# Staging the operands of a down-projection: two tiles and one row buffer, later calls, low parts on VectorE

## The chip, the core and the metric

One core of one Trainium2 chip runs the whole program. The metric is device time in microseconds; the kernel before took 2233.93 us, the median of 3 runs.

## What is computed

A trunk of two layers over 1040 tokens (16 meta tokens ahead of 1024), 1024 channels, in float32. Layer 0 mixes tokens with a gated short convolution, layer 1 with a gated linear recurrence; behind each stands a gated MLP (FFN, inner width 2816) with a convolution of width 3 between up-projection and activation.

```python
def short_conv_mixer(x, w_in, conv_w, w_out):
    b_gate, c_gate, v = jnp.split(x @ w_in, 3, axis=-1)
    return (b_gate * causal_dwconv(c_gate * v, conv_w)) @ w_out

def rglru_block(...):
    g_branch, r_branch = jnp.split(x @ w_in, 2, axis=-1)
    u = causal_dwconv(r_branch, conv_w) + conv_b
    # r, i: sigmoid gates of u by block-diagonal weights
    # a = exp(-8 r softplus(-lam)); hs = scan of a, sqrt(1-a*a) * i * u
    return (hs * gelu(g_branch)) @ w_out

def conv_gated_mlp(x, w_up, conv_w, w_down):
    g, v = jnp.split(causal_dwconv(x @ w_up, conv_w), 2, axis=-1)
    return (silu(g) * v) @ w_down

for layer in range(2):
    h = h + mixer[layer](rms_norm(h))
    h = h + conv_gated_mlp(rms_norm(h))
out = rms_norm(h)[:, 16:]
```

## The kernel before

Channels lie in partitions, tokens in columns, 1040 in four banks of 260. Each float32 product is made of three matmuls in the fp32r type: an operand is split into a high part, cast by ScalarE, and a low part, the difference, so that high x high, high x low and low x high are summed in PSUM. Weights are split so by split_weights (L225 to L229: cast L227, subtract L228 on VectorE). SyncE loads them, mostly 256 or 512 KB at a time; run() and its helper ahead (L290 to L312) make the split pieces up to six ahead of the product that uses them, and load up to nine ahead.

There are four stages: short convolution (sc), FFN 0 (zff0), recurrent block (rg, zrg), FFN 1 (zff1). Each has an up-projection (up, L398 to L504) and a down-projection (down, L507 to L616). An up-projection goes unit by unit, a unit being two output tiles of 128 channels; most units take seven products p = 1 to 7 (in the way of Strassen) in the order 1, 2, 6, 5, 7, 4, 3, with product 1 of the next unit between 7 and 4. Each is 24 matmuls. Products 1, 6, 7, 4 add up in one bank pair "a", which ScalarE copies out on the way (L461, L465, L468), 2 in "b" and 5, 3 in "c" (VectorE, L473 among them). So product 4 can begin only when the copy L468 has read the bank behind product 7; in the last unit no product of another unit stands between these two. What a unit yields, convolved and gated, is written to DRAM (the tensors zsc, zff, zrg). PSUM holds four such tiles.

A down-projection takes its operands back, in groups of k: 8 in the short convolution, 5 and 5 in the recurrent block, 9, 7, 6 and 9, 10, 3 in the two FFNs, 62 in all. bring(k) (L515 to L523) issues a DMA on GpSimd's queue from DRAM into a staging tile, casts the high part on ScalarE (L521) and subtracts the low part on GpSimd (L522). Staging tiles are s13 and s24 (one buffer each, which the up-projection's weights use too, through L261 on the same queue) and a buffer "zs" from the pool of nine rows that the convolutions, gates and results use as well. The first group's k all go to rows; from the second group on k modulo 3 chooses. The calls that bring the first group, two k each, are hooked in after the products of the last unit, from product 1 on; the rest are brought within the group before, one per step. pair (L539 to L569) then makes two output tiles over a group: its results leave PSUM by VectorE's copies (L565, first group) or adds (L563), and a GpSimd DMA (L567) adds the residual. Recurrent gates (L780 to L804) take a matmul per bank (L790), sigmoids (L793) and other ScalarE functions, then on VectorE a chain L798, L802, the scan L803 and the product L804, whose result goes to DRAM (zrg); the tenth is made inside the first group of its down-projection.

The order on TensorE is the program's own; that on the other engines is set by the tile framework's scheduler, and each engine runs its instructions in that order. A DMA issue that waits for its buffer holds back what stands behind it on its queue.

Of the kernel before, what the change touches and what calls it, by code (L numbers as in the profile page):

```python
# [7 lines left out]
FP32 = mybir.dt.float32  # L8
F32R = mybir.dt.float32r
AF = mybir.ActivationFunctionType  # L10
ALU = mybir.AluOpType
# [22 lines left out]
NJ = KD // 2  # L34
# [35 lines left out]
def unit_order(u0, n):  # L70


    out = [(u0, 1)]
    for u in range(u0, n):
        out += [(u, p) for p in (2, 6, 5, 7)]
        if u < n - 1:
            out.append((u + 1, 1))
        out += [(u, p) for p in (4, 3)]
    return out
# [57 lines left out]
def trunk_kernel(ctx: ExitStack, tc: tile.TileContext, xt: bass.AP, small: bass.AP, ws: bass.AP, out: bass.AP):  # L137
    nc = tc.nc
# [11 lines left out]
    def row(name, dtype=FP32):  # L150
        return rpool.tile([P, T], dtype, tag="row", name=name, padded_shape=[P, T + 4])
# [16 lines left out]
    def col(name, i):  # L168
        at, n = SMALL[name]
        return cv[:, at + i:at + i + 1]  # L170
# [5 lines left out]
    rn = keep.tile([P, T], FP32, name="rn")  # L176
# [54 lines left out]
    def staging(tag):  # L231
        return wpool.tile([P, T], FP32, tag=tag, name=tag, bufs=1)
# [18 lines left out]
    def unit_pieces(q):  # L251


        st = {}

        def load(p):
            if p == 1:
                st[11] = fetch(q, 3 * C, C)
                st["s13"] = staging("s13")
                nc.sync.dma_start(st["s13"][:, :2 * C], block(q)[:, 2 * C:4 * C])  # L260
                nc.gpsimd.dma_start(st["s13"][:, :2 * C], block(q)[:, C:3 * C], accum_op=ALU.add)  # L261
            elif p == 2:
                st[12] = fetch(q, 0, C)
            elif p == 4:
                st[22] = fetch(q, C, C)

        def make(p):
            if p == 6:
                s24 = st["s24"] = staging("s24")
                nc.vector.tensor_add(s24[:, :C], st["s13"][:, :C], st[11])  # L270
                nc.vector.tensor_add(s24[:, C:2 * C], s24[:, :C], st[12])
            src = {
                1: lambda: st[11], 2: lambda: st[12], 4: lambda: st[22],
                5: lambda: st["s13"][:, :C], 7: lambda: st["s13"][:, C:2 * C],
                6: lambda: st["s24"][:, :C], 3: lambda: st["s24"][:, C:2 * C],
            }[p]()
            return split_weights(src, C)

        return {p: (lambda p=p: load(p), lambda p=p: make(p)) for p in ORDER}
# [4 lines left out]
    def step(pieces, fn):  # L284
        program.append((pieces, fn))

    def hook(fn):
        program.append((None, fn))

    def run():  # L290
        pieces = []
        for ps, _ in program:
            pieces += [p for p in ps or () if p not in pieces]
        made, state = {}, {"loaded": 0, "made": 0}

        def ahead(i, last, loads=9, makes=6):
            while state["loaded"] < min(max(i + loads, last + 1), len(pieces)):
                pieces[state["loaded"]][0]()
                state["loaded"] += 1
            while state["made"] < min(max(i + makes, last + 1), len(pieces)):  # L300
                p = pieces[state["made"]]
                made[p] = p[1]()
                state["made"] += 1

        for q, (ps, fn) in enumerate(program):
            if ps is None:
                fn()
                continue
            if ps:
                at = [pieces.index(p) for p in ps]  # L310
                ahead(min(at), max(at), *((3, 2) if min(at) < NJ - 1 else (5, 4) if min(at) < NJ else ()))
            fn(*[made[p] for p in ps])  # L312


# [83 lines left out]
    def up(name, layer, units, tok, n_plain, new_out, finish, between=lambda u: None, in_last=(), n_late=0, before_pair=lambda j: None, after_plain=lambda js: None):  # L398


        a, n = tok
# [30 lines left out]
        def product(u, p, w):  # L432
            which = {1: "a", 6: "a", 7: "a", 4: "a", 2: "b", 5: "c", 3: "c"}[p]
            first, last = p in (1, 2, 5), p in (4, 2, 3)
            if first:
                bank[u, which] = banks()
            ps = bank[u, which]
            hi, lo = w
            for j in range(NJ):
                c = slice(j * P, (j + 1) * P)  # L440
                xh, xl = X[p, j]
                for b in range(2):
                    t = slice(b * n, (b + 1) * n)
                    for r, (wt, x) in enumerate(((hi, xh), (hi, xl), (lo, xh))):
                        nc.tensor.matmul(  # L445
                            ps[:, b, :n], lhsT=wt[:, c], rhs=x[:, t],
                            start=(first and j == 0 and r == 0), stop=(last and j == NJ - 1 and r == 2),
                            skip_group_check=True,
                        )
            with tc.high_priority():  # L450
                take(u, p)
# [23 lines left out]
        def finish_unit(u):  # L475
            for k in "abc":
                bank.pop((u, k), None)
            finish(u, *(t for t, _ in outs.pop(u)))
# [9 lines left out]
                    hook(lambda: after_plain(range(2, NJ)))  # L488
        pieces = {u: unit_pieces(qs[u]) for u in range(n_plain, len(units))}
        calls = list(in_last)  # L490
        for u, p in unit_order(n_plain, len(units)):
            step((pieces[u][p],), lambda w, u=u, p=p: product(u, p, w))
            if u == len(units) - 1 and len(calls) > n_late:
                hook(calls.pop(0))
            if (u, p) == (n_plain, 6):
                yield
                for v in range(n_plain):
                    between(v)
                    hook(lambda v=v: finish_unit(v))
            if p == 3:  # L500
                between(u)
                hook(lambda u=u: finish_unit(u))
# [4 lines left out]
    def down(name, layer, groups, zd, tok, residual, ready, at=lambda g, m: None):  # L507


        a, n = tok  # L510
        e = a + 4 * n
        z, h = {}, {}
        starts = [sum(groups[:g]) for g in range(len(groups) + 1)]

        def bring(k):  # L515
            which = 2 if k < groups[0] else k % 3
            s = row("zs") if which == 2 else staging(("s13", "s24")[which])
            nc.gpsimd.dma_start(s[:, a:e], zd[k][:, a:e])
            hi = xpool.tile([P, 4 * ALL[1]], F32R, tag="x", name="zh")
            lo = xpool.tile([P, 4 * ALL[1]], F32R, tag="x", name="zl")  # L520
            nc.scalar.copy(hi[:, a:e], s[:, a:e])  # L521
            nc.gpsimd.tensor_sub(lo[:, a:e], s[:, a:e], hi[:, a:e].bitcast(FP32))  # L522
            z[k] = hi, lo  # L523

        def bring_some(ks):
# [281 lines left out]
    def add_gates(i):  # L807
# [6 lines left out]
        at=lambda g, m: add_gates(NR - 1) if (g, m) == (0, 0) else None,  # L814
# [2 lines left out]

    def give_out(m, h, t, c):
        last = c == 3
        engine = nc.vector  # L820
        engine.scalar_tensor_tensor(h[m][:, t], h[m][:, t], col("g_fin", m), rn[:, t], op0=ALU.mult, op1=ALU.mult)  # L821
        queue = (nc.sync, nc.scalar)[m % 2] if last else nc.sync
        queue.dma_start(out[:, m, t.start - N_META:t.stop - N_META], h[m][:, t])

# [83 lines left out]
```

## Time and profile before

| what | value |
|---|---|
| median of 3 runs (lowest, highest) | 2233.93 us (2231.8, 2234.08) |
| the profiled execution | 2231.59 us, span 2229.8 us |
| mean granted TensorE clock | 0.982 |
| TensorE (PE) busy | 2130.3 us, 96% of the span |
| VectorE (DVE) busy | 1491.7 us, 67% |
| ScalarE (ACT) busy | 999.0 us, 45% |
| GpSimd (POOL) busy | 322.7 us, 14% |
| DMA, mean | 116 GB/s |

The profiled execution lies 0.1% below the median. Busy times are sums over the span; the stages differ, so the waits have to be read where they stand. The line of the clock, PEclk, gives the granted clock in tenths of full; 2.4 GHz is full, and the other level is 1.2 GHz.

### The profile page before, as it was taken

How to read it: one execution, taken by the hardware profiler on the slowest of the kernel's cores; microseconds unless marked ns; L12 is line 12 of the kernel's file. 1: busy time of each engine (PE TensorE's matmuls, PEld its weight loads, DVE VectorE, ACT ScalarE, POOL GpSimd, SP SyncE). 2: the span in 40 equal slices, each digit the busy share in tenths (PEclk: the TensorE clock that was granted, in tenths of full speed). 3: DMA queues.
4: the chain of work that ended last, by engine and by line, in shares of the span. 5: the costliest groups of instructions: out<-in, count | busy, mean ns of one | idle time of the engine just before them, and what ended most of it. 6: DMA issues, size and time to landing. Idle time of an engine off the chain costs nothing. (4 is left out here: it accounts for less than half of the span.)

```text
span 2229.8 us, 41117 instructions
## 1 busy us (share of the span) xinstructions
PE 2130.3 (96%) x17364; PEld 2117.0 (95%) x17364; DVE 1491.7 (67%) x1796; ACT 999.0 (45%) x1437; POOL 322.7 (14%) x316
## 2 busy tenths in 40 slices
PE   8999999899999989999999997899999999989998
PEld 8999999899999989999999997899999999889998
DVE  8866755787788774224877776497877877853226
ACT  8433343544444442112568886174444444522113
POOL 0000410000000044220001124200000000343102
PEclk9999999999999999999999999999999999989999
DMA  5434544344444454442223334632444444544312
GB/s 175 109 108 116 172 120 111 91 116 117 121 122 114 115 189 129 122 105 72 92 74 107 100 103 121 143 128 77 118 128 115 119 109 128 176 129 122 95 34 77
DMA packets 99546, 257.61 MB, mean 116 GB/s; under 512 B 11040, under 2 KB 19104, under 8 KB 99360
## 3 DMA queue, kind: packets, MB, share of 16 engines
q1 hardware_dynamic: 76320, 172.52, 23.2%
q0 software_dynamic: 22320, 81.73, 17.4%
q8 instruction: 136, 2.23, 0.4%
q10 hardware_dynamic: 720, 0.73, 0.1%
q14 instruction: 50, 0.41, 0.1%
HBM read 205.20 MB, written 49.73 MB: 114 GB/s over the span
## 5 line engine op out<-in xcount | busy, mean ns | idle before, releaser
L445 PE MATMUL ps<-x,whi 128*128 128x260 f32 (+1 forms) x6832 | 1248.0, 285 | 38.7 <-ACT cin L468 20.6
L445 PEld LDWEIGHTS ps<-x,whi 128*128 128x128 f32 x6832 | 1067.0, 190 | 41.2 <-ACT cin L468 21.4
L445 PE MATMUL ps<-x,wlo 128*128 128x260 f32 (+1 forms) x3416 | 972.0, 285 | 0.0
L445 PEld LDWEIGHTS ps<-x,wlo 128*128 128x128 f32 x3416 | 649.9, 190 | 0.0
L228 DVE TENSOR_TENSOR wlo<-wraw,whi 128x512 fp32r<-128x512 f32 (+1 forms) x337 | 276.5, 824 | 434.5 <-ACT whi L227 434.5
L555 PE MATMUL ps<-zh,whi 128*128 128x260 f32 (+2 forms) x1888 | 537.1, 284 | 27.9 <-DVE h L565 17.6
L555 PE MATMUL ps<-zl,whi 128*128 128x260 f32 (+2 forms) x1888 | 535.6, 284 | 0.0
L555 PE MATMUL ps<-zh,wlo 128*128 128x260 f32 (+2 forms) x1888 | 535.4, 284 | 0.0
L227 ACT CAST whi<-wraw 128x512 fp32r<-128x512 f32 (+1 forms) x337 | 203.2, 606 | 603.2 <-PE ps L555 367.5
L555 PEld LDWEIGHTS ps<-zh,whi 128*128 128x128 f32 x1888 | 359.2, 190 | 29.8 <-DVE h L565 12.3
L555 PEld LDWEIGHTS ps<-zl,whi 128*128 128x128 f32 x1888 | 359.3, 190 | 0.0
L555 PEld LDWEIGHTS ps<-zh,wlo 128*128 128x128 f32 x1888 | 359.1, 190 | 0.0
L227 ACT CAST whi<-s 128x512 fp32r<-128x512 f32 x244 | 150.5, 618 | 263.2 <-PE ps L445 191.8
L261 POOL DMA_DIRECT2D s<-in_ws x61 | 53.0, 868 | 1217.8 <-DMA s<-in_ws 520.0
L623 DVE SCALAR_TENSOR_TENSOR t<-cin,cv,t 128x1040 f32<-128x1040 f32 (+1 forms) x176 | 222.8, 1325 | 8.7 <-ACT t L742 6.8
L228 DVE TENSOR_TENSOR wlo<-s,whi 128x512 fp32r<-128x512 f32 x244 | 173.1, 714 | 45.5 <-ACT whi L227 45.0
L742 ACT ACTIVATE t<-cin,cv 128x1040 f32<-128x1040 f32 (+1 forms) x88 | 97.4, 1152 | 88.0 <-DVE cin L739 88.0
L418 PE MATMUL ps<-x,whi 128*128 128x260 f32 (+1 forms) x640 | 117.0, 285 | 8.6 <-ACT whi L227 8.6
L522 POOL TENSOR_TENSOR zl<-zs,zh 128x1040 fp32r<-128x1040 f32 (+2 forms) x41 | 111.3, 2724 | 74.8 <-ACT zh L521 61.7
L739 DVE SCALAR_TENSOR_TENSOR cin<-cin,rn 128x1040 f32<-128x1040 f32 (+1 forms) x88 | 109.2, 1244 | 0.1
L418 PEld LDWEIGHTS ps<-x,whi 128*128 128x128 f32 x640 | 99.9, 191 | 8.6 <-ACT whi L227 8.6
L418 PE MATMUL ps<-x,wlo 128*128 128x260 f32 (+1 forms) x320 | 91.1, 285 | 0.4 <-DVE wlo L228 0.4
(131 smaller groups left out, 1842.3 us busy)
## 6 DMA issues: line engine op xcount, KB each, us to landing
wraw<-in_ws SPq DMA_DIRECT2D x317, 256.0 KB, 3.3
s<-in_ws SPq DMA_DIRECT2D x61, 512.0 KB, 3.6
s<-in_ws POOLq DMA_DIRECT2D x61, 512.0 KB, 5.8
zff<-t SPq DMA_DIRECT2D x22, 520.0 KB, 2.7
zff<-t SPq DMA_DIRECT2D x22, 512.0 KB, 2.7
h<-h SPq DMA_DIRECT2D x16, 520.0 KB, 3.4
zs<-zff POOLq DMA_DIRECT2D x13, 520.0 KB, 5.0
zs<-zff POOLq DMA_DIRECT2D x13, 512.0 KB, 6.1
```

The costliest lines, as they stand in the source:

```text
L227: nc.scalar.copy(hi[:, :n], src)
L228: nc.vector.tensor_sub(lo[:, :n], src, hi[:, :n].bitcast(FP32))
L261: nc.gpsimd.dma_start(st["s13"][:, :2 * C], block(q)[:, C:3 * C], accum_op=ALU.add)
L418: nc.tensor.matmul(ps[:, s, :n], lhsT=wt, rhs=x[:, t], start=(j == 0 and k == 0), stop=(j == NJ - 1 and k == 5),)
L445: nc.tensor.matmul(ps[:, b, :n], lhsT=wt[:, c], rhs=x[:, t], start=(first and j == 0 and r == 0), stop=(last and j == NJ - 1 and r == 2), ...
L522: nc.gpsimd.tensor_sub(lo[:, a:e], s[:, a:e], hi[:, a:e].bitcast(FP32))
L555: nc.tensor.matmul(ps[:, s, :n], lhsT=w[wt][:, k], rhs=x[:, t], start=(i == 0 and q == 0), stop=(i == k1 - 1 and q == 2),)
L623: nc.vector.scalar_tensor_tensor(t[:, a:e], cin[:, a + s:e + s], col(wname, at + k), t[:, a:e], op0=ALU.mult, op1=ALU.add)
L739: nc.vector.scalar_tensor_tensor(c, c, sign, rn[:, a:e], op0=ALU.mult, op1=ALU.mult)
L742: nc.scalar.activation(t[:, oa:], cin[:, oa + 2:e + 2], AF.Copy, scale=col(wconv, at + 2))
```

## The change

All operands of a down-projection are staged by k modulo 3: two tiles and a row buffer, the first group's too. The calls that bring the first group come after the last of the products 2, 6, 5, 7, 4, 3 of the last unit, one call per product, as many products as there are calls (with five calls 6, 5, 7, 4, 3; with three 7, 4, 3); in the short convolution one of the four calls comes behind the last unit, as before. The low part is subtracted on VectorE. Besides, at the start a fourth piece of weights is made one step earlier, and an engine is named directly in the output step.

```diff
--- before.py
+++ after.py
@@ -308,7 +308,7 @@
                 continue
             if ps:
                 at = [pieces.index(p) for p in ps]
-                ahead(min(at), max(at), *((3, 2) if min(at) < NJ - 1 else (5, 4) if min(at) < NJ else ()))
+                ahead(min(at), max(at), *((3, 2) if min(at) < NJ - 1 else (5, 5) if min(at) < NJ else ()))
             fn(*[made[p] for p in ps])
 
 
@@ -488,9 +488,10 @@
                     hook(lambda: after_plain(range(2, NJ)))
         pieces = {u: unit_pieces(qs[u]) for u in range(n_plain, len(units))}
         calls = list(in_last)
+        spots = (2, 6, 5, 7, 4, 3)[-len(calls):]
         for u, p in unit_order(n_plain, len(units)):
             step((pieces[u][p],), lambda w, u=u, p=p: product(u, p, w))
-            if u == len(units) - 1 and len(calls) > n_late:
+            if u == len(units) - 1 and p in spots and len(calls) > n_late:
                 hook(calls.pop(0))
             if (u, p) == (n_plain, 6):
                 yield
@@ -513,13 +514,13 @@
         starts = [sum(groups[:g]) for g in range(len(groups) + 1)]
 
         def bring(k):
-            which = 2 if k < groups[0] else k % 3
+            which = k % 3
             s = row("zs") if which == 2 else staging(("s13", "s24")[which])
             nc.gpsimd.dma_start(s[:, a:e], zd[k][:, a:e])
             hi = xpool.tile([P, 4 * ALL[1]], F32R, tag="x", name="zh")
             lo = xpool.tile([P, 4 * ALL[1]], F32R, tag="x", name="zl")
             nc.scalar.copy(hi[:, a:e], s[:, a:e])
-            nc.gpsimd.tensor_sub(lo[:, a:e], s[:, a:e], hi[:, a:e].bitcast(FP32))
+            nc.vector.tensor_sub(lo[:, a:e], s[:, a:e], hi[:, a:e].bitcast(FP32))
             z[k] = hi, lo
 
         def bring_some(ks):
@@ -817,8 +818,7 @@
 
     def give_out(m, h, t, c):
         last = c == 3
-        engine = nc.vector
-        engine.scalar_tensor_tensor(h[m][:, t], h[m][:, t], col("g_fin", m), rn[:, t], op0=ALU.mult, op1=ALU.mult)
+        nc.vector.scalar_tensor_tensor(h[m][:, t], h[m][:, t], col("g_fin", m), rn[:, t], op0=ALU.mult, op1=ALU.mult)
         queue = (nc.sync, nc.scalar)[m % 2] if last else nc.sync
         queue.dma_start(out[:, m, t.start - N_META:t.stop - N_META], h[m][:, t])
```

Behind the second hunk the lines of the changed kernel are one higher: the DMA is L519, the cast L522, the subtract L523, the bank copy L566, the scan L804.

GpSimd's queue at the first group of FFN 1's down-projection; the number in front in a tensor's name (zff1_0) is the layer, the next is k. Before:

```order
L518 DMA zs_21212<-zff1_0_147 128x1024
L518 DMA zs_21218<-zff1_1_148 128x1024
L518 DMA s13_21859<-zff1_9_156 128x1024
L522 TENSOR_TENSOR zl_21215<-zs_21212,zh_21214 128x1024
L522 TENSOR_TENSOR zl_21221<-zs_21218,zh_21220 128x1024
L518 DMA s24_21919<-zff1_10_157 128x1024
L518 DMA zs_21331<-zff1_2_149 128x1024
L518 DMA zs_21337<-zff1_3_150 128x1024
L518 DMA zs_21374<-zff1_4_151 128x1024
L518 DMA zs_21380<-zff1_5_152 128x1024
L522 TENSOR_TENSOR zl_21334<-zs_21331,zh_21333 128x1024
```

With the change:

```order
L519 DMA s13_21350<-zff1_0_147 128x1024
L519 DMA s13_21399<-zff1_3_150 128x1024
L519 DMA s24_21356<-zff1_1_148 128x1024
L519 DMA zs_21393<-zff1_2_149 128x1024
L519 DMA s24_21438<-zff1_4_151 128x1024
L519 DMA zs_21444<-zff1_5_152 128x1024
L519 DMA zs_21524<-zff1_8_155 128x1024
L519 DMA s13_21481<-zff1_6_153 128x1024
L519 DMA s24_21487<-zff1_7_154 128x1024
```

The subtracts are gone from the queue, k = 0, 1 and 2 go to three different buffers, and k = 3 and the later ones stand in line for the buffers of those ahead of them, k = 3 in front of k = 1.

ScalarE's order at the same place, from the copy behind product 6 to the copy L468 behind product 7, before product 4 can begin. Before:

```order
L465 COPY cin_21210<-ps_21185 128x2x258
L745 ACTIVATE t_21287<-t_21287 128x1024
L521 CAST zh_21333<-zs_21331 128x1024
L227 CAST whi_21431<-wraw_21299 128x512
L521 CAST zh_21339<-zs_21337 128x1024
L227 CAST whi_21470<-wraw_21343 128x512
L521 CAST zh_21376<-zs_21374 128x1024
L468 COPY cin_21459<-ps_21185 128x2x258
```

With the change:

```order
L465 COPY cin_21210<-ps_21185 128x2x258
L522 CAST zh_21358<-s24_21356 128x1024
L746 ACTIVATE t_21275<-t_21275 128x1024
L227 CAST whi_21407<-wraw_21287 128x512
L522 CAST zh_21395<-zs_21393 128x1024
L227 CAST whi_21452<-wraw_21319 128x512
L468 COPY cin_21435<-ps_21185 128x2x258
```

Three casts of staged operands (zh, of k = 2, 3 and 4) stood ahead of L468; now two do, of k = 1 and 2.

VectorE's order in the first group of the recurrent block's down-projection, around the tenth gate's scan and the bank copies (h) of the second and third pair of output tiles. Before:

```order
L803 SCALAR_TENSOR_TENSOR th_15077<-ra_15075,ix_15076 128x1040
L565 COPY h_15235<-ps_15111 128x516
L565 COPY h_15235<-ps_15118 128x516
L565 COPY h_15251<-ps_15125 128x516
L565 COPY h_15251<-ps_15132 128x516
L804 TENSOR_TENSOR g_14815<-th_15077,g_14815 128x1032
L228 TENSOR_TENSOR wlo_15232<-wraw_15069,whi_15231 128x512
L228 TENSOR_TENSOR wlo_15276<-wraw_15105,whi_15275 128x256
L228 TENSOR_TENSOR wlo_15340<-wraw_15169,whi_15339 128x512
L228 TENSOR_TENSOR wlo_15400<-wraw_15229,whi_15399 128x512
L565 COPY h_15403<-ps_15279 128x516
```

With the change, from the last copy of the second pair on:

```order
L566 COPY h_15251<-ps_15132 128x516
L804 SCALAR_TENSOR_TENSOR th_15077<-ra_15075,ix_15076 128x1040
L228 TENSOR_TENSOR wlo_15232<-wraw_15069,whi_15231 128x512
L805 TENSOR_TENSOR g_14785<-th_15077,g_14785 128x1032
L228 TENSOR_TENSOR wlo_15276<-wraw_15105,whi_15275 128x256
L523 TENSOR_TENSOR zl_15334<-zs_15331,zh_15333 128x1032
L228 TENSOR_TENSOR wlo_15340<-wraw_15169,whi_15339 128x512
L523 TENSOR_TENSOR zl_15394<-s13_15391,zh_15393 128x1032
L566 COPY h_15403<-ps_15279 128x516
```

The scan, which stood ahead of the second pair's copies, comes behind them, and two low parts (zl, of k = 8 and 9 of this block) stand ahead of the third pair's.

## Rows read from the trace of the kernel before

**Rows 1.** Timeline of TensorE: start, us, engine, instruction [idle before <- releaser].

```profile
258.38 0.51 PE L445 MATMUL ps<-x,whi 128*128 128x260 f32 x2 [2.04 <-ACT c L468]
269.35 0.39 PE L555 MATMUL ps<-zh,whi 128*128 128x260 f32 x1 [1.10 <-DVE c L473]
833.08 0.80 PE L445 MATMUL ps<-x,whi 128*128 128x260 f32 x2 [10.08 <-ACT cin L468]
1347.51 0.80 PE L445 MATMUL ps<-x,whi 128*128 128x260 f32 x2 [9.57 <-ACT g L468]
1401.05 0.58 PE L555 MATMUL ps<-zh,whi 128*128 128x258 f32 x1 [9.19 <-DVE h L565]
1421.30 0.36 PE L555 MATMUL ps<-zh,whi 128*128 128x258 f32 x1 [3.41 <-DVE h L565]
1947.30 0.80 PE L445 MATMUL ps<-x,whi 128*128 128x258 f32 x2 [5.57 <-ACT cin L468]
1966.38 0.58 PE L555 MATMUL ps<-zh,whi 128*128 128x256 f32 x1 [8.85 <-DVE cin L473]
```

**Rows 2.** Waits of TensorE: us in total, times, longest us.

```profile
PE ps L790 <- ACT ra L793: 7.4, 8, 2.7
```

**Rows 3.** Windows of TensorE: us, PE busy (x), PEclk, DMA share, GB/s.

```profile
258.30:266.20 7.90, 7.82 (x51) 0.78 0.90 237
833.00:842.00 9.00, 8.92 (x51) 0.65 0.43 135
1347.40:1355.20 7.80, 7.69 (x49) 0.75 0.46 135
1401.00:1418.00 17.00, 16.84 (x120) 0.86 0.63 164
1947.30:1955.30 8.00, 8.00 (x49) 0.70 0.78 279
1966.40:1972.60 6.20, 6.20 (x29) 0.51 0.35 113
```

**Rows 4.** Timeline of ScalarE before product 4 of the first FFN.

```profile
824.15 0.61 ACT L227 CAST whi<-wraw 128x512 fp32r<-128x512 f32 x1
831.48 1.06 ACT L521 CAST zh<-zs 128x1040 fp32r<-128x1040 f32 x1 [6.71 <-DMA zs<-zff]
832.44 0.59 ACT L468 COPY cin<-ps 128x520 f32<-128x520 f32 x1
```

**Rows 5.** Timeline of GpSimd, end of both FFN up-projections.

```profile
820.39 6.15 POOL L522 TENSOR_TENSOR zl<-zs,zh 128x1040 fp32r<-128x1040 f32 x1 [4.12 <-ACT zh L521]
...
1925.96 0.54 POOL L518 DMA_DIRECT2D s<-zff  x1 [14.39 <-DVE wlo L228]
...
1952.62 9.38 POOL L522 TENSOR_TENSOR zl<-zs,zh 128x1024 fp32r<-128x1024 f32 x4
```

**Rows 6.** Timeline of VectorE in the same stretch of the second FFN.

```profile
1952.89 11.68 DVE L228 TENSOR_TENSOR wlo<-wraw,whi 128x256 fp32r<-128x256 f32 x1 [2.54 <-ACT whi L227]
```

**Rows 7.** Lines of VectorE by form: busy us, mean ns | idle before.

```profile
L748 DVE TENSOR_TENSOR t<-t 128x1040 f32<-128x1040 f32 x22 | 27.1, 1234 | 0.0
```

**Rows 8.** Costliest groups of the page: busy us, mean ns | idle before.

```profile
L522 POOL TENSOR_TENSOR zl<-zs,zh 128x1040 fp32r<-128x1040 f32 (+2 forms) x41 | 111.3, 2724 | 74.8 <-ACT zh L521 61.7
```

**Rows 9.** DMAs: KB, median us to landing; and the tile zs, min/median/max.

```profile
s<-zff POOLq DMA_DIRECT2D x9, 520.0 KB, 4.0
...
DMA to landing us min/median/max: 3.4/5.3/9.4
```

**Rows 10.** Lines of ScalarE by form: busy us, mean ns | idle before.

```profile
L745 ACT ACTIVATE t<-t 128x1024 f32<-128x1024 f32 x22 | 23.4, 1062 | 18.8 <-DVE t L623 18.8
```

**Rows 11.** Timeline of VectorE, recurrent block's first down-projection group.

```profile
1389.33 2.62 DVE L798 SCALAR_TENSOR_TENSOR th<-u,th 128x1040 f32<-128x1040 f32 x1 [10.41 <-ACT u L797]
...
1398.08 2.32 DVE L803 TENSOR_TENSOR_SCAN th<-ra,ix 128x1040 f32<-128x1040 f32 x1
```

**Rows 12.** Costliest groups of the page, TensorE.

```profile
L445 PE MATMUL ps<-x,whi 128*128 128x260 f32 (+1 forms) x6832 | 1248.0, 285 | 38.7 <-ACT cin L468 20.6
```

## The prediction

> **What bounds the kernel now.** TensorE does. I read the granted clock first (0.982 over the span), then every idle stretch of TensorE on its timeline, then for each the engine that released it, followed back on that engine's own timeline, and last the windows behind the stretches for the clock. Its busy time leaves 99.5 us of the span; the reader is to see in [rows 1] that eight waits hold 49.8 of it and that all of them stand where an up-projection hands over to its down-projection or just behind. To them comes one wait of 2.7 at the start of the gates [rows 2]. Together 52.5 us are within this change's reach. The second thing to see is the clock: after these waits PEclk reads 0.51 to 0.86 of full, which is a stretch at 1.2 GHz before it is back at 2.4 [rows 3]. The loss is length times (1 - PEclk): 7.9 x 0.22 = 1.7, 9.0 x 0.35 = 3.15, 7.8 x 0.25 = 1.95, 17 x 0.14 = 2.4, 8 x 0.30 = 2.4 and 6.2 x 0.49 = 3.0, in sum 14.6. So the stake is 67 us, 3% of the span. The product matmuls themselves are untouched: TensorE's order is the same.
>
> **Why the waits are there.** Two mechanisms. First: between product 7 and product 4 of the last unit TensorE needs its bank copied by ScalarE (L468). In [rows 4] that copy, 0.59 long, stands in ScalarE's order behind a cast of a staged operand that idled 6.71 for its DMA. The DMA was late because GpSimd issues it and GpSimd was subtracting: 6.15 for one low part in [rows 5]. Second: while GpSimd subtracts, VectorE crawls. In [rows 5] it runs four subtracts back to back from 1952.62 to 1962.0, and another behind them; in [rows 6] VectorE's subtract of 128x256, begun at 1952.89, takes 11.68. A full-width subtract of two SBUF tiles takes 1.23 with VectorE to itself [rows 7], so this quarter-width one should take about 0.3. The bank copy L473 stands behind it, and TensorE waits 8.85.
>
> **The change part by part.** *Low parts to VectorE.* 62 subtracts leave GpSimd: 41 of them took 111.3 [rows 8], and the other 21 at the same 2.7 some 57. That is 168 us of an engine that bounds nothing, but it ends both mechanisms' source. They cost VectorE 62 x 1.23 = 76 us; it is busy 67%, so on average there is room, and where they stand ahead of something that TensorE waits for is counted below.
>
> *Staging in two tiles and one row buffer.* k = 0, 1, 2 go to s13, s24 and a row, k = 3 back to s13, which first needs k = 0 landed, cast and subtracted. GpSimd issues k = 3 ahead of k = 1 (order above), so k = 1 waits for that too, and for VectorE to free s24. What a landing costs decides: the issues into these buffers took 4.0 at the median, those into rows 3.4 at least, 5.3 at the median and 9.4 at most [rows 9]. I take L = 4.4, nearer the 4.0 as two or three and not four transfers are now under way at once; 3.4 and 9.4 are the ends.
>
> *Second FFN.* s13 comes free at 1925.96 [rows 5]. Then k = 0 lands (L), cast 1.06 and subtract 1.23, two half-width VectorE instructions that free s24 (estimate 2 x 0.62 by [rows 7]), an issue (0.5), k = 1 lands (L). On ScalarE then stand cast 1.06, a gate activation 1.06 [rows 10], weight cast 0.61, cast of k = 2 1.06, weight cast 0.61, and L468 0.59 (durations of [rows 4]), 5.0 in all. L468 ends at 1925.96 + 2L + 2.3 + 1.2 + 0.5 + 5.0 = 1935 + 2L. TensorE comes to it at 1947.30 - 5.57 = 1941.73, so it waits 2L - 6.7 = **2.1**, for 5.57. The 8.85 behind it goes to about 0.5: VectorE has three low parts and two weight parts, some 5 us, ahead of L473, against products 4 and 3 with about 5.8 us. Of 14.42 go 11.8; of the clock's 5.4 I leave 1.2, less than the 1.7 that waits of 2.04 and 1.10 cost in [rows 1, 3], and save 4.2. **16.0.**
>
> *First FFN.* The same chain with rows of 1040: I take 2.5 for the 10.08, and 0.4 for a bank turn. 7.2 of idle and 2.0 of the clock's 3.15: **9.2.**
>
> *Recurrent block.* The gates' first wait falls from 2.7 to the 0.67 that the other seven average ((7.4 - 2.7)/7, [rows 2]), since no cast stands ahead of ScalarE's table loads: 2.0. The 9.57 becomes 1.8, for of the staged operands only k = 0's cast, landed long before, is left ahead of L468: 7.8. The 9.19: VectorE went from 1389.33 to 1400.3 through a chain of four, first and last in [rows 11], ahead of the bank copies: 11.0 us. Now the scan (2.32) comes behind the copies, the other three, undisturbed, at 1.23, 0.62 and 1.23 are 3.1, and three low parts come in, 3.7: 6.8. That saves 4.2, the wait is 5.0. The 3.41 grows: the bank copies of m = 4 now stand behind the low part of k = 9 (order above), whose data go scan, product, DRAM and back; scan and product come later by some 2.2 against TensorE. I take 5.6; between 3.4, if the landing is in time, and 7.9, if all of the 4.5 that was gained ahead of it is lost. Of the clock's 4.35 I save 1.1, since waits of five remain. 11.8 + 1.1: **12.9.**
>
> *Short convolution.* 2.04 becomes 1.3, 1.10 goes, and the clock's 1.7 halves; the later calls may cost up to 1 in a new wait for k = 6: **2.5**, between 0 and 3.5.
>
> *The fourth weight piece made one earlier, and the engine name in the output step.* Nothing: TensorE's waits at the start are for the first pieces and the fourth is not among them; the second edit issues the same instruction.
>
> *Groups in the middle.* Their staging was k modulo 3 before already; a low part is now VectorE's 1.23 beside products of 24 matmuls, 6.8 us each at 0.285 [rows 12]. Nothing, covered by those products; the price if that cover is gone is the rival C.
>
> **Sum:** 16.0 + 9.2 + 12.9 + 2.5 = 40.6. The profiled execution took 2231.59 (span 2229.8), so 2191.0; the median of the runs is 2.3 above it, and what is compared is that median: 2233.9 - 40.6 gives 2193, which I round down to **2192** for VectorE instructions that quicken elsewhere. The case's own ends: with landings at 5.3 each FFN wait is 1.8 longer, 9.19 stays (4.2), the wait behind it is 7.9 (2.3), the short convolution gives nothing (2.5) and 2 more of clock stay, so 26 are saved. With landings at 3.4 the FFN waits shrink to a bank turn of 0.5 (3.6), 3.41 does not grow (2.2), the 5.0 is 2 (3.0), and 7 of clock and short convolution come back: 57. So 2177 to 2208.
>
> **A rule against the trace.** [Rows 5, 6] show one VectorE subtract of 11.68 across five GpSimd subtracts, so its wait was several of them long. The Trainium skill, page "SBUF — State Buffer", section "Who interferes with whom", says that a VectorE instruction with two SBUF inputs and a GpSimd one that reads SBUF exclude each other for a whole instruction, whoever issues first. By that rule one VectorE instruction waits for one GpSimd instruction at most, so the 8.85 would shrink by some 2.4 only and the result would be near 2198; the measured 11.68 decides, and the sum stands without it.
>
> **The rivals.** *A, more: every wait shrinks to a bank turn* and VectorE's relief shows in places where I counted nothing. For it: the two mechanisms explain nearly all of the 52.5. Against: the serial staging and the low part of k = 9 are in the new order. Over 57 saved, about 2172.
>
> *B, half is given back: the staging in series is slow.* If landings take 6 to 8, as rows above the median of 5.3 did [rows 9], each FFN wait grows by 2 x (L - 4.4), 3.2 to 7.2; the 9.19 stays (4.2), the next wait reaches 7.9 (2.3), the short convolution gives nothing (2.5), and a clock loss of 1 to 4 stays. 16 to 27 of the 40.6 go: 14 to 24 saved, 2209 to 2220. For it: issues stand in GpSimd's order behind ones that wait. Against: fewer transfers at once.
>
> *C, slower: VectorE stands at low parts ahead of bank copies.* VectorE works in order; where a low part waits for its landing and cast, the copies that free the down-projection's banks wait behind it, which GpSimd's subtract never did to them. The new order has a low part within four instructions ahead of a bank copy at nine places, two of which are in my sum. If at the other seven the landing is asked for only as the bank ends, each costs 4.0 + 1.06 + 1.23 = 6.3, with 0.85 of clock 7.1, in sum 50: 2243. It decides from 5.8 per place. Against: the calls come a whole product (6.8) ahead or more.
>
> *D, the waits only move*, from copies behind casts to casts behind landings, in equal measure: no change, 2234. Landings of 9.3, as the slowest row [rows 9], would do it in the FFNs (two times 2L - 6.7 is 23.8, and 0.9 of bank turns, against 24.5 now); the other two blocks would have to go the same way. Against: in both, other terms than landings carry the gain.
>
> **How the numbers follow.** Forecast 0.64, A 0.08, B 0.19, C 0.05, D 0.04. From no change a measurement of this kernel can tell about 0.2%, 4.5 us. Faster by more: forecast, A and B, 0.91. Within: D, 0.04. Slower: C, 0.05. The range begins at 2175, which leaves out most of A, and ends at 2219, nearly all of B; left out are C, D and some 0.08 of A and B.
>
> **What would show it.** GpSimd's busy time falls by about 168 and VectorE's rises by less than 76, as the stretched subtracts shrink. No VectorE instruction in these stages takes several times its usual length. The waits for L468 in the FFNs are near 2; the one for L473 is nearly gone; of the two for bank copies in the recurrent block the first is near 5 and the second grows. The forecast is wrong if a low part that waits on VectorE releases TensorE in the middle groups, if landings into s13 and s24 take over 6, or if the clock falls as long after waits of 2 as after waits of 10.

## The result and the profile after

The changed kernel took 2181.85 us, the median of 4 runs (2179.13 to 2184.17), against 2233.3 of the kernel before in the same comparison. The ratio is 0.977, with a 95% interval of 0.9753 to 0.9787: 51.5 us faster. The prediction was 2192, in a range of 2175 to 2219. Direction and range were right, the size was 10 us short.

The profiled executions part by 49.3 us of span, from 2229.8 to 2180.5. The page says of the changed kernel:

```profile
PE 2121.6 (97%) x17364; PEld 2108.4 (97%) x17364; DVE 1489.8 (68%) x1858; ACT 999.5 (46%) x1437; POOL 163.5 (7%) x254
```

TensorE's busy time fell by 8.7 and its idle time by 40.6. The 8.7 is clock: over the whole span TensorE worked 45.8 us at 1.2 GHz before and 29.0 after, which at half speed is 22.9 and 14.5 lost, 8.4 less. The timeline of TensorE in the changed kernel, at the places that answer to [rows 1]:

```profile
258.25 0.50 PE L445 MATMUL ps<-x,whi 128*128 128x260 f32 x2 [1.08 <-ACT c L468]
...
282.53 0.39 PE L556 MATMUL ps<-zl,whi 128*128 128x260 f32 x1 [0.85 <-DVE zl L523]
...
820.79 0.51 PE L445 MATMUL ps<-x,whi 128*128 128x260 f32 x2 [1.95 <-ACT cin L468]
...
1323.01 0.51 PE L445 MATMUL ps<-x,whi 128*128 128x260 f32 x2 [0.71 <-ACT g L468]
...
1369.76 0.58 PE L556 MATMUL ps<-zh,whi 128*128 128x258 f32 x1 [4.50 <-DVE h L566]
...
1388.85 0.45 PE L556 MATMUL ps<-zh,whi 128*128 128x258 f32 x1 [1.96 <-DVE h L566]
...
1911.46 0.50 PE L445 MATMUL ps<-x,whi 128*128 128x258 f32 x2 [1.08 <-ACT cin L468]
...
1920.04 0.39 PE L556 MATMUL ps<-zh,whi 128*128 128x256 f32 x1 [0.41 <-DVE cin L473]
```

The eight waits of 49.81 are now these eight of 12.54, one of them new (0.85, for a low part in the short convolution; three later runs with the same edits there do not show it). Of the gates' eight waits [rows 2] the one of 2.7 is gone; they average 0.7 (in total, times, longest):

```profile
PE ps L791 <- ACT ra L794: 5.4, 8, 1.0
```

The windows behind the waits answer to [rows 3] (us, PE busy, PEclk, DMA share, GB/s):

```profile
820.80:828.80 8.00, 8.00 (x54) 0.79 0.79 253
1369.70:1386.80 17.10, 17.04 (x120) 0.84 0.63 163
1388.85:1396.85 8.00, 8.00 (x54) 0.79 0.90 196
1911.40:1919.40 8.00, 7.94 (x66) 1.00 0.98 331
```

Behind a wait of 1.08 the clock stays at 2.4 GHz, behind one of 1.95 a part of the window is at 1.2 GHz. The length of the wait does not settle it alone: in two of the runs below PEclk is 1.00 over the 8 us behind waits of 2.03 (1918.20, low parts on VectorE) and 2.15 (1368.57, another buffer). Length times (1 - PEclk) gives 1.7, 2.7 and 1.7 in the three that are below full, 6.1, for the 14.6 of before; in the short convolution, from 258.25 to 266.25, PEclk is 1.00 too.

VectorE's lines by operation show what the low parts cost there:

```profile
L523 DVE TENSOR_TENSOR zl<-s,zh 128x1040 fp32r<-128x1040 f32 (+2 forms) x43 | 52.5, 1229 | 28.6 <-ACT zh L522 28.5
L523 DVE TENSOR_TENSOR zl<-zs,zh 128x1040 fp32r<-128x1040 f32 (+2 forms) x19 | 23.4, 1231 | 26.9 <-ACT zh L522 26.7
```

That is 75.9 us more work for VectorE, and yet its busy time fell, from 1491.7 to 1489.8: without the subtracts beside it, its other instructions, the same ones as before, shrank by about 78. The run below that moves the low parts and nothing else shows the same: 1490.5 busy, with 76.7 of low parts in it.

### The profile page after: what moved, and what is told of

Same layout as the page of the kernel before. It is cut to its first block, busy times and chain, and to the rows that moved or that the text cites. A ratio compares the mean times of both kernels' runs of the same rounds, so it can differ in the third digit from the quotient of the medians.

```text
span 2180.5 us, 41094 instructions
## 1 busy us (share of the span) xinstructions
PE 2121.6 (97%) x17364; PEld 2108.4 (97%) x17364; DVE 1489.8 (68%) x1858; ACT 999.5 (46%) x1437; POOL 163.5 (7%) x254
## 5 line engine op out<-in xcount | busy, mean ns | idle before, releaser
L228 DVE TENSOR_TENSOR wlo<-wraw,whi 128x512 fp32r<-128x512 f32 (+1 forms) x337 | 224.8, 671 | 364.7 <-ACT whi L227 364.4
L624 DVE SCALAR_TENSOR_TENSOR t<-cin,cv,t 128x1040 f32<-128x1040 f32 (+1 forms) x176 | 216.7, 1288 | 5.0 <-ACT t L743 3.3
L228 DVE TENSOR_TENSOR wlo<-s,whi 128x512 fp32r<-128x512 f32 x244 | 166.3, 686 | 44.6 <-ACT whi L227 44.0
L463 DVE TENSOR_TENSOR cin<-ps,cin 128x520 f32<-128x520 f32 (+1 forms) x51 | 35.6, 698 | 63.8 <-PE ps L445 63.8
```

The lines of the kernel that those rows point to most:

```text
L228: nc.vector.tensor_sub(lo[:, :n], src, hi[:, :n].bitcast(FP32))
L463: nc.vector.tensor_add(quarter(0, 0), gb, quarter(0, 0))
L624: nc.vector.scalar_tensor_tensor(t[:, a:e], cin[:, a + s:e + s], col(wname, at + k), t[:, a:e], op0=ALU.mult, op1=ALU.add)
```

## The experiments

Every comparison below is against runs of the kernel before on the same chip, whose medians were 2230.2 to 2230.8. Theory 1 throughout: GpSimd's subtracts are the cause, by holding back the staging issues behind them and by stretching VectorE's instructions. Theory 2: the place counts at which operands are staged and called.

### Low parts on VectorE, nothing else

```diff
-            nc.gpsimd.tensor_sub(lo[:, a:e], s[:, a:e], hi[:, a:e].bitcast(FP32))
+            nc.vector.tensor_sub(lo[:, a:e], s[:, a:e], hi[:, a:e].bitcast(FP32))
```

> Kernel before with one edit: the low part is subtracted on VectorE; staging in rows and early calls stay. Theory 1 (GpSimd's subtracts are the cause: they hold back the staging issues behind them and stretch VectorE's instructions): most of the 51.5 us gained comes with this edit alone, 2185 to 2195; the waits of 10.08 and 5.57 for L468 fall under 2.5, the 8.85 for L473 under 1, no VectorE subtract of 128x256 over 1 us at the end of FFN 1's up-projection. Theory 2 (what counts is when and where the operands are staged: casts of early-called operands stand ahead of L468): under a third of it, 2216 to 2234; the L468 waits stay above 5.

Measured: 2189.49, ratio 0.9822 (0.9805 to 0.9838), a gain of 41.3 between the medians, four fifths of the whole. The FFNs' waits for L468 are 0.85 and 2.03, and their waits for L473 are under 0.75. Theory 1 carries this much. But one large wait did not go, the recurrent block's for L468, 9.57 before [rows 1]:

```profile
1327.95 0.80 PE L445 MATMUL ps<-x,whi 128*128 128x260 f32 x2 [8.64 <-ACT g L468]
```

ScalarE's timeline of that run says why:

```profile
1322.68 1.05 ACT L521 CAST zh<-zs 128x1032 fp32r<-128x1032 f32 x1 [2.38 <-DMA zs<-zrg]
1326.35 1.05 ACT L521 CAST zh<-zs 128x1032 fp32r<-128x1032 f32 x1 [2.62 <-DMA zs<-zrg]
1327.31 0.58 ACT L468 COPY g<-ps 128x520 f32<-128x520 f32 x1
```

and GpSimd's, where no subtract of a low part is left:

```profile
1318.98 0.58 POOL L518 DMA_DIRECT2D zs<-zrg  x1 [7.90 <-issue]
1320.21 0.54 POOL L518 DMA_DIRECT2D zs<-zrg  x1 [0.65 <-DVE u L623]
```

Two casts stand ahead of the bank copy, and their rows are issued late: the second issue is released by VectorE's L623, which gives up a row of the pool that gates and operands share. The kernel before has the same picture there: its second issue, at 1338.96, is released by L623 too. Here theory 2 is right.

### Low parts back on GpSimd

```diff
-            nc.vector.tensor_sub(lo[:, a:e], s[:, a:e], hi[:, a:e].bitcast(FP32))
+            nc.gpsimd.tensor_sub(lo[:, a:e], s[:, a:e], hi[:, a:e].bitcast(FP32))
```

(in the changed kernel)

> Changed kernel with the low part back on GpSimd; three staging buffers and late calls stay. Theory 1: the subtracts block the issues and stretch VectorE again; with only two or three buffers in turn the chain per k is 1.2 us longer, so the waits are at least those of before: 2225 to 2250. Theory 2: keeps over two thirds of the gain, 2182 to 2199.

Measured: 2218.91, ratio 0.9947 (0.9932 to 0.9962): 11.9 faster than before, which neither theory had. The two halves nearly add: 41.3 + 11.9 = 53.2 against 51.5 for both together. TensorE's timeline parts the two kinds of waits:

```profile
823.50 0.51 PE L445 MATMUL ps<-x,whi 128*128 128x260 f32 x2 [1.73 <-ACT cin L468]
...
834.15 0.80 PE L445 MATMUL ps<-x,whi 128*128 128x260 f32 x2 [7.51 <-DVE cin L469]
...
1395.76 0.58 PE L556 MATMUL ps<-zh,whi 128*128 128x258 f32 x1 [10.04 <-DVE h L566]
...
1949.42 0.80 PE L445 MATMUL ps<-x,whi 128*128 128x258 f32 x2 [6.43 <-DVE cin L469]
```

The waits for ScalarE's copy (1.73, and 2.35 in FFN 1) are about as short as with the low parts on VectorE (0.85 and 2.03 there); the longest ones for VectorE's additions and copies are 6 to 10, and in FFN 0 and FFN 1 they now stand at L469, where the kernel before had none. So two edits each shorten the FFNs' L468 by themselves, and only one frees VectorE. Its timeline in the first FFN, where GpSimd subtracts from 823.08 to 831.7:

```profile
826.08 3.42 DVE L749 TENSOR_TENSOR t<-t 128x1040 f32<-128x1040 f32 x1
...
833.41 0.69 DVE L469 TENSOR_TENSOR cin<-ps,cin 128x520 f32<-128x520 f32 x1
```

L749 takes 3.42 where the same instruction, L748 before, took 1.23 alone [rows 7]: 2.2 more, less than one GpSimd subtract. It is the third of four such in a row between 819.78 and 832.28: L624 took 3.51 for 1.29, L228 2.94 for 0.68, L749 3.42 and another L228 2.85 for 0.68, 8.8 us more in all, and the wait of 7.51 for L469 behind them is theirs. By the Trainium skill's rule, page "SBUF — State Buffer", section "Who interferes with whom" (two SBUF inputs on VectorE and a GpSimd instruction that reads SBUF exclude each other, one instruction at a time), that is what it should be; this stretch agrees, and the 11.68 of [rows 6], beside five subtracts, does not. Nor does a weight part L228 of 128x512 at 2057.03 of the kernel before: 5.45, beside two subtracts. L469, which reads a bank and one tile, took 0.69 when no subtract ran; in the next run it took 0.70 at 1946.46 inside a subtract that ran from 1945.32 to 1948.15.

### Staging issued by SyncE

```diff
-            nc.gpsimd.dma_start(s[:, a:e], zd[k][:, a:e])
+            nc.sync.dma_start(s[:, a:e], zd[k][:, a:e])
```

(in the kernel before; the subtracts stay on GpSimd, and no staging issue stands behind one)

> Kernel before with one edit: the staging DMAs are issued by SyncE, the subtracts stay on GpSimd. This parts the two mechanisms. Theory 1 (issues held back behind subtracts on GpSimd's queue make the L468 waits, stretched VectorE instructions make the others): the 10.08 and 5.57 for L468 fall under 2.5; a wait of 5 or more for a bank that VectorE reads stays in each FFN, and the 9.19 for L565 stays within 2; 2208 to 2225. Theory 2 (the casts stand too early in ScalarE's order, whoever issues): the L468 waits stay above 4, 2225 or more. SyncE also carries the weight loads; if those are held up behind staging issues that wait for a buffer, the time goes above 2240 with waits for whi or wlo.

Measured: 2220.54, ratio 0.9954 (0.9937 to 0.9972). The total is as theory 1 has it: with the issues freed, 10 us of the 51.5 come. The waits are only in part. Theory 1 had both FFN waits for L468 under 2.5; one fell, to 2.77:

```profile
826.63 0.50 PE L445 MATMUL ps<-x,whi 128*128 128x260 f32 x2 [2.77 <-ACT cin L468]
...
837.40 0.80 PE L445 MATMUL ps<-x,whi 128*128 128x260 f32 x2 [6.12 <-DVE cin L469]
...
1401.84 0.58 PE L555 MATMUL ps<-zh,whi 128*128 128x258 f32 x1 [7.88 <-DVE h L565]
...
1946.48 0.80 PE L445 MATMUL ps<-x,whi 128*128 128x258 f32 x2 [6.13 <-ACT cin L468]
```

In FFN 1 it stays at 6.13, as theory 2 had it. Theory 1 also had a wait of 5 or more for a bank that VectorE reads in each FFN. FFN 0 has one, 6.12, and the recurrent block keeps 7.88; in FFN 1 the longest is 0.73, though the subtracts are still on GpSimd and back to back. The weight part of 128x256 that took 11.68 in [rows 6] took 2.62 here (1953.87). So the 8.85 of the kernel before needed more than those subtracts; what let VectorE in here was not tested. SyncE's queue and VectorE there:

```profile
1934.83 0.32 SPq L518 DMA_DIRECT2D s<-zff  x1
1935.20 2.09 SPq L518 DMA_DIRECT2D zs<-zff  x4
```

```profile
1931.88 2.92 DVE L228 TENSOR_TENSOR wlo<-s,whi 128x512 fp32r<-128x512 f32 x1
```

The four rows stand behind an issue into s24, which the second group of that FFN is to use, and it goes out at 1934.83, just as the low weight part that reads s24 ends, stretched to 2.92. So in FFN 1 the late row is held back not by a subtract on its own queue but by a buffer, whose last reader is VectorE. In the kernel before it was so too: the issue into s24 went out at 1936.31, behind that weight part's end at 1936.01, when GpSimd's own subtracts had ended at 1935.46. The expectation had only the first FFN's cause.

### Early calls, and rows for the first group

```diff
-            if u == len(units) - 1 and p in spots and len(calls) > n_late:
+            if u == len(units) - 1 and len(calls) > n_late:
```

> Changed kernel with the calls hooked after the products from 1 on, as before. Theory 1: the calls' place matters little, since a staging issue waits for s13 and s24 to come free in any case: within 6 us of the changed kernel, 2176 to 2188. Theory 2: casts stand ahead of L468 again, the waits for it in the FFNs go over 4, and 2192 to 2210.

Measured: 2184.63, ratio 0.9795 (0.978 to 0.9809). The FFNs' L468 waits are 3.38 and 1.51, for 1.95 and 1.08. Three more runs below stage the FFNs as the changed kernel does; with it their waits span 1.95 to 2.79 and 1.08 to 1.30, so the calls' place is worth some 0.6 to 1.4 and 0.2 to 0.4. The recurrent block's L468 does not come back.

```diff
-            which = k % 3
+            which = 2 if k < groups[0] else k % 3
```

> Changed kernel with the first group staged in rows again (low parts on VectorE, late calls). Theory 1: rows are not the cause; 2176 to 2190, with the waits for L468 in the FFNs at most 2. Theory 2: rows compete with the results' and gates' rows, so the recurrent block's waits for bank copies go back above 9: 2195 to 2215.

Measured: 2184.22, ratio 0.9796 (0.9781 to 0.981). The FFNs' L468 waits are 0.81 and under 0.75, shorter than in the changed kernel; the recurrent block's is 1.08. So 8.64 there goes with either of the two edits. But rows do cost in that block: its waits at and behind the tenth gate are 4.12, 3.19 and 4.79. The total is theory 1's; that rows compete with the gates' rows was theory 2's, at half of the size.

### The start undone

```diff
-                ahead(min(at), max(at), *((3, 2) if min(at) < NJ - 1 else (5, 5) if min(at) < NJ else ()))
+                ahead(min(at), max(at), *((3, 2) if min(at) < NJ - 1 else (5, 4) if min(at) < NJ else ()))
```

> Changed kernel with the start undone (the fourth weight piece made as late as before). Theory 1: the start is worth nothing: 0.977 of the kernel before, within 0.002, and TensorE's first waits (before 20 us) the same to 0.3 us. Theory 2 (the start is part of the gain that the sum of waits did not hold): 0.979 or more.

Measured: 2179.06, ratio 0.977 (0.9755 to 0.9784). TensorE's waits in the first 20 us sum to 9.14 here, 9.16 in the changed kernel and 9.01 before. The start is worth nothing that can be seen.

### What is left in the recurrent block: another buffer, later calls

```diff
-            which = k % 3
+            which = (k + 1) % 2 if name == "rg_w_out" and k >= groups[0] else k % 3
```

> Changed kernel, but the recurrent block's second group goes to s13 and s24 in turn and needs no row. Theory 1 (the 4.50 that is left at the second pair's bank copies comes from k = 5, whose row comes free only when the gate's product is done, and whose cast ScalarE and so the gate's chain stand behind): 4.50 falls under 1.5, the 1.96 behind it is the same or more by at most 2; 0.974 to 0.976 of the kernel before. Theory 2 (the low parts in VectorE's order are the cost): 4.50 stays above 3.5, 0.977.

Measured: 2180.38, ratio 0.9776 (0.9761 to 0.979): no gain. Neither theory had the two waits:

```profile
1368.57 0.39 PE L556 MATMUL ps<-zh,whi 128*128 128x258 f32 x1 [2.15 <-DVE h L566]
...
1387.71 0.36 PE L556 MATMUL ps<-zh,whi 128*128 128x258 f32 x1 [4.48 <-DVE h L566]
```

The 4.50 became 2.15 and the 1.96 became 4.48: the wait only moved. The low part of k = 9 stands ahead of the third pair's copies and needs the tenth gate's result, so what the second pair gains in time the third one waits: the two sum to 6.63 here and to 6.46 in the changed kernel.

The same with the first groups of the other stages in rows:

```diff
-            which = k % 3
+            which = (k + 1) % 2 if name == "rg_w_out" and k >= groups[0] else 2 if name != "rg_w_out" and k < groups[0] else k % 3
```

> The run before this one, with the first groups of the short convolution and of the FFNs in rows. Theory 1: the FFNs' waits for L468 fall from 1.95 and 1.08 to under 1 as with rows in the changed kernel, the short convolution's 0.85 for a low part goes: 1 to 3 us under the run with two tiles in the recurrent block alone. Theory 2: more transfers at once make landings longer, no gain over it.

Measured: 2175.11, ratio 0.9754 (0.9739 to 0.9768). The gain over the run before it is 5.3, where 1 to 3 were expected. The FFNs' L468 waits are 0.96 and 0.74, for 2.58 and 1.08 in that run, and behind 0.96 PEclk stays at 1.00; a wait of 1.22 for L473 is new. The 0.85 for a low part is not there, but the run before did not have it either.

Since the wait moves between the pairs, the next edit leaves the buffers and takes the second group's calls out of the gate's way:

```diff
-                        if m > 0 and spare:
+                        if m > (2 if name == "rg_w_out" else 0) and spare:
```

> Changed kernel, but the recurrent block's second group is brought beside the third and fourth pair of output tiles, not the second and third, so that no cast and no low part stands in the tenth gate's chain. Theory 1 (both waits left there, 4.50 and 1.96, come from casts and low parts that wait for their data in ScalarE's and VectorE's order): 4.50 falls under 2, 1.96 under 0.8, 0.974 to 0.976 of the kernel before. Theory 2 (the gate's chain alone is too long for the two pairs that cover it; a wait of about 4 to 6 stays at one of them): 0.977, as before only moved.

Measured: 2171.62, ratio 0.9743 (0.9728 to 0.9759). 4.50 became 0.52, and 1.96 is not to be found above 0.3. Theory 1 holds: it was not the gate's chain that was long, but casts and low parts that waited for their data inside it.

With that edit and the rows of the run before it:

```diff
-            which = k % 3
+            which = 2 if name != "rg_w_out" and k < groups[0] else k % 3
...
-                        if m > 0 and spare:
+                        if m > (2 if name == "rg_w_out" else 0) and spare:
```

> The run before this one, with the first groups of the short convolution and of the FFNs in rows. Theory 1: both gains add, 0.972 to 0.9745 of the kernel before, with waits for L468 in the FFNs under 1 and those in the recurrent block as in the run before. Theory 2: no better than 0.9754, which rows and two tiles in the recurrent block gave.

Measured: 2166.48, ratio 0.9713 (0.97 to 0.9726), faster than both kernels and a little better than theory 1's 0.972 to 0.9745. TensorE's timeline, and VectorE's in the tenth gate:

```profile
817.96 0.51 PE L445 MATMUL ps<-x,whi 128*128 128x260 f32 x2 [0.93 <-ACT cin L468]
...
1361.15 0.39 PE L556 MATMUL ps<-zh,whi 128*128 128x258 f32 x1 [0.51 <-DVE h L566]
...
1896.33 0.50 PE L445 MATMUL ps<-x,whi 128*128 128x258 f32 x2 [0.73 <-ACT cin L468]
```

```profile
1356.90 2.32 DVE L804 TENSOR_TENSOR_SCAN th<-ra,ix 128x1040 f32<-128x1040 f32 x1
1359.26 1.23 DVE L805 TENSOR_TENSOR g<-th,g 128x1032 f32<-128x1032 f32 x1
1360.41 2.49 DVE L566 COPY h<-ps 128x516 f32<-128x516 f32 x4
```

The gate's chain now runs without a staged operand in it, ahead of the copies, and TensorE loses half a microsecond to it.

## Why the prediction was right, and where it was short

**What bounds the kernel, and the two mechanisms** were right. TensorE's waits at the handovers were the stake, and GpSimd's subtracts made most of them: moving the low parts alone gives 41.3. The text told the L468 waits by one cause, a subtract in front of an issue. The runs show three: that one in FFN 0; in FFN 1 an issue waiting for s24, whose reader on VectorE a subtract had stretched to 2.95; and rows that come free late in the recurrent block. The serial staging through two tiles and a row, which the prediction counted as a cost alone, and the later calls gain 11.9 by themselves.

**By stage**, idle and clock together, where the predicted sum was 2.5 + 9.2 + 12.9 + 16.0 = 40.6:

| stage | predicted | idle gone | clock gained | measured |
|---|---|---|---|---|
| short convolution | 2.5 | 3.14 - 1.93 = 1.2 | 1.7 - 0 | 2.9 |
| FFN 0 | 9.2 | 10.08 - 1.95 = 8.1 | 3.15 - 1.7 | 9.6 |
| recurrent block | 12.9 | 24.86 - 7.9 = 17.0 | 4.35 - 4.4 | 16.9 |
| FFN 1 | 16.0 | 14.42 - 1.49 = 12.9 | 5.4 - 0 | 18.3 |

The recurrent block's 24.86 are 2.69 of the gates and three waits of [rows 1]; the 7.9 are 0.7 for a gate and 0.71, 4.50 and 1.96. The four stages make 47.7 of the 49.3 of span; the other 1.6 were not traced. Of the 7.1 that the sum fell short, 6.3 are in the last two rows.

**FFN 1: landings.** The replay had k = 0 and k = 1 land in 4.4 each. GpSimd's timeline after, and ScalarE's:

```profile
1894.64 0.55 POOL L519 DMA_DIRECT2D s<-zff  x1 [15.47 <-DVE wlo L228]
1900.77 0.55 POOL L519 DMA_DIRECT2D s<-zff  x1 [5.58 <-DVE zl L523]
1901.96 0.53 POOL L519 DMA_DIRECT2D s<-zff  x1 [0.65 <-DVE wlo L228]
```

```profile
1898.16 1.05 ACT L522 CAST zh<-s 128x1024 fp32r<-128x1024 f32 x1 [1.14 <-DMA s<-zff]
...
1906.37 1.05 ACT L522 CAST zh<-s 128x1024 fp32r<-128x1024 f32 x1 [0.33 <-DMA s<-zff]
...
1910.82 0.58 ACT L468 COPY cin<-ps 128x516 f32<-128x516 f32 x1
```

k = 0 is issued at 1894.64 and cast at 1898.16, 3.5 later; k = 3 waits for its low part and goes out at 1900.77; k = 1, behind it, goes out at 1901.96 and is cast at 1906.37, 4.4 later; from there to the end of L468 it is 5.0, as the sum had it. The order and every duration but the first landing came as predicted: with 3.5 + 4.4 in place of twice 4.4, 2L - 6.7 is 1.2, and 1.08 was measured. And at 1.08 the clock does not fall, so all of its 5.4 came back where 4.2 was put down.

**Recurrent block: the second wait for bank copies.** The term "3.41 grows to 5.6" failed: it fell to 1.96. The step behind it was that scan and product come later against TensorE, and they did: the product L805 ended 5.7 after TensorE's restart (1375.4 - 1369.76), L804 before 2.9 (1403.9 - 1401.05). What the step left out is that the rest of the chain became shorter. Before, on GpSimd, ScalarE and VectorE:

```profile
1413.01 0.60 POOL L518 DMA_DIRECT2D s<-zrg  x1 [6.36 <-DMA zrg<-g]
```

```profile
1416.50 1.06 ACT L521 CAST zh<-s 128x1032 fp32r<-128x1032 f32 x1 [6.74 <-DMA s<-zrg]
```

```profile
1418.11 2.44 DVE L228 TENSOR_TENSOR wlo<-wraw,whi 128x512 fp32r<-128x512 f32 x1 [7.62 <-ACT whi L227]
1420.47 2.49 DVE L565 COPY h<-ps 128x516 f32<-128x516 f32 x4
```

and after:

```profile
1382.26 0.55 POOL L519 DMA_DIRECT2D s<-zrg  x1 [9.57 <-DMA zrg<-g]
```

```profile
1385.78 1.06 ACT L522 CAST zh<-s 128x1032 fp32r<-128x1032 f32 x1 [7.01 <-DMA s<-zrg]
```

```profile
1386.87 1.23 DVE L523 TENSOR_TENSOR zl<-s,zh 128x1032 fp32r<-128x1032 f32 x1 [7.38 <-ACT zh L522]
1388.02 2.49 DVE L566 COPY h<-ps 128x516 f32<-128x516 f32 x4
```

From the product's end to the issue of k = 9 it took 9.1 before and 6.9 after, and from the cast to the copies 4.0 before and 2.2 after. The wait for the cast was there before too, through a weight part stretched to 2.44 beside GpSimd's subtract, which the prediction did not follow back. 2.8 later, 2.2 and 1.8 sooner make 1.2 less, and TensorE came to the wait 0.3 later (17.1 after its restart, for 16.8): 1.5, where 1.45 was measured. The 2.2 is in the flight of the product's write to DRAM, 6.2 from issue to landing for 8.5 before. Before, two residual DMAs (L567) went out 2.1 and 0.6 ahead of it, after 4.9 and 3.7; whether that is the reason was not tested. The other terms of this block came closer: 4.50 for 5.0, 0.71 for 1.8. But the 5.0 took the start of the gate's chain on VectorE as given. ScalarE idled ahead of it for the row of k = 5, 5.14 before and 4.67 after, and the runs with later calls, where no staged operand stands there, have 0.5 in its place. Its clock gained nothing, since two waits, of 4.50 and 1.96, each still bring a stretch at 1.2 GHz.

**Readings that were off, with no effect on the sum.** The prediction gives a product of 24 matmuls 6.8, 24 times the 0.285 of [rows 12]. Matmuls overlap: in the last window above 66 take 8.0, and the product that starts at 1911.46 took 2.9. C was argued down with the 6.8; with 2.9 its cover was thinner than the text says, and C still did not come. The 6.15 of [rows 5] is not what the subtract itself takes (last section). The 62 subtracts took 165.6, not 168. And the end of 7.9 for the 3.41 gives back 4.5 where the text had gained 4.2.

**The rivals.** B's mechanism is real but small: the FFNs' L468 waits are what a chain of two landings leaves, and rows in their place take them under 1. In FFN 0 the landing of k = 1 took 5.5 in the changed kernel, not 4.4, and 6.1 to 6.4 in three later runs, whose waits are 2.47 to 2.79; k = 0 landed in 3.8, so the 2.5 held. C did not come: one wait for a low part appeared, of 0.85, in one profile. D did not come. A was partly right: in the short convolution and the FFNs every wait left is under 2, and VectorE's relief was 78, but nearly all of the gain lies in places that the sum had.

**What would show it.** GpSimd's busy time fell by 159 (168 was expected; one of its ten products L795 became longer, 27.6 us in all for 24.4). VectorE's did not rise at all. L624 at 3.48 for a mean of 1.29 is the one VectorE instruction found at several times its length (last section). The rule of the Trainium skill weighed above, "Who interferes with whom" on the page "SBUF — State Buffer", would have put the result near 2198; 0.41 is left of the 8.85, so the gain went by the measured 11.68. That this one instruction was kept out so long is shown by one trace only; beside subtracts that again ran back to back, in the run with SyncE's issues, it took 2.62.

## What to carry to other kernels

Read a wait back through every queue it passes: here one copy on ScalarE waited for a cast, the cast for a DMA, the DMA for its place behind a subtract on the issuing engine or for a buffer's last reader on a third one. An elementwise instruction on an idle engine is not free when it stretches the instructions of a busy one (1.23 us to 3.42 above) and stands in a queue with transfers: the same 62 subtracts cost 166 us on GpSimd and 76 on VectorE, and VectorE was no busier for it. And when a wait only moves as a buffer is changed, look for instructions in the chain that need not be there yet; here another buffer gave nothing (ratio 0.9776 for 0.977) and later calls some 6 us (0.9743; the two intervals just overlap, but the waits of 4.50 and 1.96 are gone from the trace).

## What was not expected of the hardware

Landings into rows became longer while those into the two tiles stayed short. The medians after, from the DMA view (KB, us to landing):

```profile
s<-zff POOLq DMA_DIRECT2D x15, 520.0 KB, 4.6
zs<-zff POOLq DMA_DIRECT2D x7, 520.0 KB, 7.8
```

The median from DRAM to a row of either FFN is 7.8, for 5.0 and 6.1 before. Rows are now issued right behind another transfer; whether that is the reason was not tested. None of TensorE's waits shown above goes back to such a row, so it costs nothing here.

The stretching works both ways, and an engine can be kept out for several instructions of the other. The subtract of 6.15 in [rows 5] stood while VectorE ran five instructions back to back, from 820.05 to 824.30; the two subtracts behind it took 2.4 each, so some 3.7 of the 6.15 reads as waiting, and the issue behind it was late by that too. In the changed kernel GpSimd's product of the ninth gate took 5.62 from 1333.83 on, where the other nine took 2.4 to 2.5. VectorE ran back to back until 1337.15, and its next instruction, the first of three L624, took 3.48 in its turn, to 1340.55; the other two took 1.30. The same product took 5.56 with another buffer and 5.68 with later calls.
